# A two-block transformer kernel on one core: the gated linear recurrence's states chunk by chunk, its gates' silu apart from the copies out of PSUM, and half GEMMs written between the parts of a pair

## The chip, the core and the metric

The kernel runs on one core of a Trainium2 chip. The core has five engines that run side by side: TensorE (PE for matmuls, PEld for its weight loads), VectorE (DVE), ScalarE (ACT), GpSimd (POOL) and SyncE (SP, which only issues DMAs here). Each engine takes its own instructions strictly in order and waits on semaphores for the others. Matmul results land in PSUM, everything else is in SBUF. The metric is the device time of one execution in microseconds (us), as the median over runs.

## The reference, cut to what matters

The whole computation is two transformer blocks in float32. The first has two layers over 512 latent and 256 context positions of width 1024; the second has one layer. The change lies in one branch of the first block, which runs once in each of its two layers: a gated linear recurrence with four heads of 64 keys and 64 values, run forward and backward over the positions.

```
a     = cumsum(log f) inside a chunk
S_new = exp(a_last) * S + sum_s (k * exp(a_last - a))^T v      # one state per chunk, 64 x 64 per head
out   = (q * exp(a)) S  +  (scores inside the chunk) v
y     = rms_norm(out_forward + out_backward) * silu(gate)
```

The kernel uses chunks of 32 positions, so there are 24 chunks per direction (8 of the context, then 16 of the latent positions). The layer's other branches (attention, Fourier, convolution) have gates of their own: each is a GEMM of the normalised input with 256 columns of `w_in`, passed through silu. Layer 0 needs both streams (768 positions); layer 1 needs the branch outputs of the 512 latent positions alone.

## The kernel before, in words

Every float32 GEMM is done as three matmuls of a high and a low part (`mm3`, L187 to L191; the parts are made by `split`, L193 to L195, on ACT and DVE). Weights come as units of 256 columns: a DMA brings 1 MB, ACT writes the high parts (`wh`), DVE the low parts (`wl`). `Ahead.more` prepares the next unit while the current one is in use; there is room for about one unit of `wh` and `wl` at a time. `cp_gemm` (L457) computes one half of a unit, 128 columns, for all positions: 24 matmuls 512 wide (`gl`) and, in layer 0, 24 matmuls 256 wide (`gc`). A half is what this text calls a half GEMM.

`hgrn` (from L737) does the recurrence for two pairs of heads, j = 0 and j = 1. For each it computes the forget gates (`kk`, `lf`), and for j = 0 also the queries `q` and the values `ivt`. Then `hgrn_pair` (L807) handles the pair in four parts: two directions, each with a context part of 2 tiles (256 positions) and a latent part of 4 tiles (512 positions). A part (`hgrn_part`, L834) has two steps:

- Step one, on DVE and ACT alone: a running sum over each chunk (L843, L845), then exponentials and products that give `kt`, `F`, `Qd`, `Kd` (L853 to L889).
- Step two, with PE: `kt` is transposed (L894) and copied out (`KT`, L896); matmuls give each chunk's own update of the state (L906), three ACT instructions copy the updates into the state tile `S` (L912, L914); matmuls give the scores inside the chunks (L923), which DVE masks and adds up into `sc` (L931 to L939). Two of the four update results lie in PSUM tiles of the tag `sm`, of which there are two, and the scores need the same two.

After the two parts of a direction `hgrn_scan` (L941) turns the updates into states. Before the change the state tile is laid out as [128, 64 values, 24 chunks], with the chunks side by side; the decays are spread to 1536 columns by one copy (L946), and one scan instruction over 1536 columns (L948) runs the recurrence, with a zero decay at each row's first chunk. `hgrn_out` (L950) then multiplies `sc` with the values and the decayed queries with the states of the chunk before (both L976), squares and normalises the result (L983 to L986), and transposes bring it back (L830) to be multiplied into `y` (L832).

The gates are written around the pair. For j = 0 these are `y[4:6]` ahead of the pair, `y[2:4]` after its four parts and scans, `y[6:8]` after `hgrn_out`. For j = 1 these are `y[0:2]` after the parts, and one more unit after `hgrn_out` whose GEMM result DVE multiplies into `y[0:2]` (L803). `gate` (L993) runs two half GEMMs and lets ACT apply silu on the way out of PSUM (L998). `fill` runs one step of an independent filler, matmuls over `w_mod` (L398).

The order of instructions on each engine is not the order of the source. The framework that builds the program keeps, on every engine, a list of instructions whose inputs will be ready by its own estimate, and takes the one written first among those; so the place in the source is a rank. `ACT_TABLE_LOAD` instructions, which exchange ACT's function table between silu, sigmoid, exp and ln, are not in the source; the compiler adds them.

Of the kernel before, what the change touches and what calls it, by code (L numbers as in the profile page):

```python
# [147 lines left out]
class K:  # L148
# [588 lines left out]
    def hgrn(self, l, w_in, need, hp):  # L737
        nc = self.nc
        segs = ((0, 512), (512, 256))
        nt = 6 if need else 4  # L740
        self.hgmask = hp.tile([128, 192], I32, tag="hgmask", name="hgmask", bufs=1)
        nc.scalar.dma_start(self.hgmask, self.I["c_hgmask"])
        self.scanmask = hp.tile([128, 512], F32, tag="scanmask", name="scanmask", bufs=1)
        nc.scalar.dma_start(self.scanmask, self.I["c_scanmask"])
        ivt = hp.tile([128, 6, 256], F32, tag="ivt", name="ivt", bufs=1)
        qs = [None, None]
        for j in range(2):
            u = self.first if l == j == 0 else self.units.take()
            kk = [hp.tile([128, T], F32, tag="kk", name="kk") for _ in range(2)]
            lf = [hp.tile([128, T], F32, tag="lf", name="lf") for _ in range(2)]  # L750

            def evac(d, p, c0, n):
                nc.scalar.activation(kk[d][:, c0:c0 + n], p, AF.Sigmoid, scale=-1.0)
                nc.scalar.activation(lf[d][:, c0:c0 + n], p, AF.Sigmoid)

            for d in range(2):
                evac(d, self.cp_gemm(u[d], need_lat=False, tag=("mm" if j else "sm"))[1], 512, 256)
            if j == 0:
                ps = self.lat_gemm(u, ("mm", "mm"))
                self.units.more()  # L760
                for d, p in enumerate(ps):
                    evac(d, p, 0, 512)
            else:
                for d in range(2):
                    evac(d, self.cp_gemm(u[d], need_ctx=False, more=d == 1)[0], 0, 512)
            self.fill()
            if j == 0:
                u = self.units.take()
                for jj in range(2):
                    pl, pc = self.cp_gemm(u[jj], need_ctx=need, more=jj == 1)  # L770
                    q = hp.tile([128, T], F32, tag="q", name="q")
                    nc.scalar.activation(q[:, 0:512], pl, AF.Silu)
                    if need:
                        nc.scalar.activation(q[:, 512:768], pc, AF.Silu)
                    qs[jj] = q
                self.fill()
                for i, ps in self.tp_panel():
                    nc.scalar.activation(ivt[:, i, :], ps, AF.Copy)
                    if i in (1, 4):
                        self.fill()  # L780
            for d in range(2):
                sc_, bi = self.lscale[:, l, d, j:j + 1], self.lbias[:, l, d, j:j + 1]
                nc.scalar.activation(lf[d], lf[d], AF.Ln, scale=sc_, bias=bi)
                if l:
                    nc.vector.tensor_scalar(kk[d], kk[d], sc_, None, ALU.mult)
            self.dbg(f"lf{l}{j}0", lf[0]); self.dbg(f"lf{l}{j}1", lf[1])
            if j == 0:
                self.gate(self.y[4:6], need)
            steps = self.hgrn_pair(l, j, kk, lf, qs[j], ivt, need, nt, hp)
            next(steps)  # L790
            if j == 0:
                self.gate(self.y[2:4], need)
                next(steps)
                self.gate(self.y[6:8], need)
                next(steps, None)
            else:
                self.gate(self.y[0:2], need)
                next(steps)
                u = self.units.take()
                for jj in range(2):  # L800
                    for p, (c0, n) in zip(self.cp_gemm(u[jj], need_ctx=need, more=jj == 1), self.segs(need)):
                        ys = self.y[jj][:, c0:c0 + n]
                        nc.vector.tensor_tensor(ys, ys, p, ALU.mult)  # L803
                self.fill()
                next(steps, None)

    def hgrn_pair(self, l, j, kk, lf, q, ivt, need, nt, hp):  # L807

        nc = self.nc
        sc = hp.tile([128, 6, 2, 32], F32, tag="sc", name="sc", bufs=1)  # L810
        Ss = [hp.tile([128, 64, 24], F32, tag="S", name="S") for _ in range(2)]
        decs = [hp.tile([128, 24], F32, tag="dec", name="dec") for _ in range(2)]
        parts = [self.hgrn_part(d, c0, n, kk[d], lf[d], q, ivt, need or c0 == 0, j, Ss[d], decs[d], sc, hp)
                 for d in range(2) for c0, n in ((512, 256), (0, 512))]
# [2 lines left out]
        for n in range(4):  # L817
            if n < 3:
                next(parts[n + 1])
            next(parts[n], None)  # L820
            if n % 2:
                self.hgrn_scan(Ss[n // 2], decs[n // 2], hp)
        yield
        on = self.hgrn_out(lf, Ss, sc, ivt, nt, j, hp)
        yield
        y = self.y[4 + j]
        for (i0, n) in ((0, 4), (4, 2))[:2 if need else 1]:
            tr = self.psum("tr", [128, 128 * n])
# [5 lines left out]
    def hgrn_part(self, d, c0, n, kk, lf, q, ivt, out, j, St, dec, sc, hp):  # L834
# [66 lines left out]
        for ii in range(ntile):  # L901
            i = c0 // 128 + ii
            for A in range(4):
                rs = slice(32 * A, 32 * A + 32)
                for p in range(2):
                    nc.tensor.matmul(ups[A][64 * p:64 * p + 64, ii], KT[rs, 128 * ii + 64 * p:128 * ii + 64 * p + 64],  # L906
                                     ivt[rs, i, 128 * j + 64 * p:128 * j + 64 * p + 64], start=True, stop=True)
        sv = St[:, :, o0:o0 + nch]
        if d:
            sv = sv[:, :, ::-1]  # L910
        sv = sv.rearrange("p v (i a) -> p a i v", a=4)
        nc.scalar.activation(sv[:, 0:2], u2[:, :, :64 * ntile].rearrange("p a (i v) -> p a i v", v=64), AF.Copy)  # L912
        for A in (2, 3):
            nc.scalar.activation(sv[:, A], ups[A], AF.Copy)  # L914
# [23 lines left out]
                nc.vector.tensor_reduce(s1, M.rearrange("p i (l t) -> p i t l", l=3), AX.X, ALU.add)  # L938
                nc.vector.tensor_tensor(so, so, s1, ALU.add)  # L939

    def hgrn_scan(self, St, dec, hp):  # L941

        nc = self.nc
        nc.vector.memset(dec[:, 0:1], 0.0)
        de = hp.tile([128, 64, 24], F32, tag="de", name="de", bufs=1)
        nc.vector.tensor_copy(de, dec[:, None, :].to_broadcast([128, 64, 24]))  # L946
        S2 = St.rearrange("p v c -> p (v c)")
        nc.vector.tensor_tensor_scan(S2, de.rearrange("p v c -> p (v c)"), S2, 0.0, ALU.mult, ALU.add)  # L948

    def hgrn_out(self, Qas, Ss, sc, ivt, nt, j, hp):  # L950

# [2 lines left out]
        for i in range(nt):  # L954
            todo = {}
            for A in range(4):
                qsl = slice(32 * A, 32 * A + 32)
                for p in range(2):
                    t = [(sc[qsl, i, p, :], ivt[qsl, i, 128 * j + 64 * p:128 * j + 64 * p + 64])]
                    for d in range(2):  # L960
                        if i >= 4:
                            c = 4 * (i - 4) + A
                            c = c if d == 0 else 7 - c
                        else:
                            c = 4 * i + A
                            c = 8 + (c if d == 0 else 15 - c)
                        if c == 0:
                            continue
                        x0 = 128 * i + 32 * A
                        t.append((Qas[d][64 * p:64 * p + 64, x0:x0 + 32], Ss[d][64 * p:64 * p + 64, :, c - 1]))  # L970
                    todo[A, p] = t

            for n_ in range(3):
# [16 lines left out]
    def segs(self, need):  # L990
        return ((0, 512), (512, 256)) if need else ((0, 512),)

    def gate(self, tiles, need):  # L993

        u = self.units.take()
        for j in range(2):
            for p, (c0, n) in zip(self.cp_gemm(u[j], need_ctx=need, more=j == 1), self.segs(need)):
                self.nc.scalar.activation(tiles[j][:, c0:c0 + n], p, AF.Silu)  # L998
        self.fill()

    def attention(self, l, w_in, need, ap):
        nc = self.nc
# [1086 lines left out]
```

## Time and profile before

| what | value |
|---|---|
| median of 3 runs | 1754.92 us (1752.55 to 1758.75) |
| the profiled execution's own time | 1756.17 us |
| its span, first to last instruction | 1754.4 us |
| PE busy | 1630.6 us (93%) |
| DVE busy | 1017.9 us (58%) |
| ACT busy | 872.1 us (50%) |
| mean granted TensorE clock | 0.965 |

PE is busy for most of the span; the rest, some 124 us, is time in which PE had nothing it could start. [...] An engine's idle time is listed with the instruction that ended it, so that a row "A <- B" reads: A waited, and B let it go.

### The profile page before, as it was taken

To read this page: it belongs to the slowest core of one execution; us is meant where nothing else is said; L and a number is where in the kernel's file an instruction comes from. 1 tells how busy PE (TensorE), PEld (TensorE's weight loads), DVE (VectorE), ACT (ScalarE), POOL (GpSimd) and SP (SyncE) were. 2 spreads that over 40 slices of the span, in tenths; PEclk is the share of its full clock that TensorE was granted. 3 is DMA by queue.
4 is the path that set the end of the run, shared out by engine and by line. 5 is a ranking of instruction groups with operands and counts; after the bars stand their busy time and mean duration, and the time that the engine had idled before them with its cause. 6 is when DMAs were issued, how large, how long until landed. Compare 5 with 4: busy or idle time off the path is not lost. (4 is left out here: it accounts for less than half of the span.)

```text
span 1754.4 us, 31468 instructions
## 1 busy us (share of the span) xinstructions
PE 1630.6 (93%) x12731; PEld 1334.6 (76%) x12731; DVE 1017.9 (58%) x2133; ACT 872.1 (50%) x1754; POOL 220.4 (13%) x226
## 2 busy tenths in 40 slices
PE   5998979999999887999999889999999999999998
PEld 3876758877778675879787668777788888888886
DVE  4635473676565546586777896778766633333223
ACT  4844662553467474455556732666555533333222
POOL 2100001101230000110213443002100011111000
PEclk8998989999999898999999997999999999999999
DMA  9231203202454111213764234102724533332431
GB/s 361 104 122 51 96 27 130 98 1 67 166 161 168 51 49 56 96 49 96 265 208 135 73 90 97 37 25 70 230 85 168 181 88 99 99 99 85 156 109 72
DMA packets 162574, 193.86 MB, mean 111 GB/s; under 512 B 15054, under 2 KB 124910, under 8 KB 160252
## 3 DMA queue, kind: packets, MB, share of 16 engines
q1 hardware_dynamic: 156604, 183.37, 32.2%
q10 hardware_dynamic: 5824, 8.47, 1.7%
q8 instruction: 100, 1.64, 0.4%
q14 instruction: 46, 0.38, 0.1%
HBM read 175.28 MB, written 13.66 MB: 108 GB/s over the span
## 5 line engine op out<-in xcount | busy, mean ns | idle before, releaser
L194 ACT ACTIVATE wh<-raw 128x512 fp32r<-128x512 f32 (+1 forms) x458 | 282.3, 628 | 435.6 <-PE mm L190 161.2
L195 DVE TENSOR_TENSOR wl<-raw,wh 128x512 fp32r<-128x512 f32 x416 | 285.1, 699 | 357.7 <-ACT wh L194 344.7
L189 PE MATMUL mm<-xh,wh 128*128 128x512 f32 x520 | 208.4, 401 | 1.4 <-ACT acc L1627 1.0
L191 PE MATMUL mm<-xh,wl 128*128 128x512 f32 x520 | 208.1, 401 | 0.0
L190 PE MATMUL mm<-xl,wh 128*128 128x512 f32 x520 | 207.8, 400 | 0.0
L191 PE MATMUL gl<-xh,wl 128*128 128x512 f32 (+1 forms) x480 | 182.4, 381 | 6.0 <-DVE wl L195 3.9
L189 PE MATMUL gl<-xh,wh 128*128 128x512 f32 (+1 forms) x480 | 181.7, 379 | 3.5 <-ACT y L998 2.5
L190 PE MATMUL gl<-xl,wh 128*128 128x512 f32 (+1 forms) x480 | 180.6, 377 | 0.1
L189 PEld LDWEIGHTS mm<-xh,wh 128*128 128x128 f32 x520 | 100.6, 193 | 23.0 <-ACT acc L1627 1.9
L191 PEld LDWEIGHTS mm<-xh,wl 128*128 128x128 f32 x520 | 100.4, 193 | 20.5
L190 PEld LDWEIGHTS mm<-xl,wh 128*128 128x128 f32 x520 | 100.3, 193 | 20.5
L189 PEld LDWEIGHTS gl<-xh,wh 128*128 128x128 f32 x480 | 93.4, 195 | 22.8 <-issue 3.4
L191 PEld LDWEIGHTS gl<-xh,wl 128*128 128x128 f32 x480 | 93.9, 196 | 19.6 <-DVE wl L195 5.2
L190 PEld LDWEIGHTS gl<-xl,wh 128*128 128x128 f32 x480 | 93.5, 195 | 14.3 <-issue 1.1
L195 POOL TENSOR_TENSOR wl<-raw,wh 128x512 fp32r<-128x512 f32 x42 | 58.1, 1388 | 110.8 <-ACT wh L194 74.4
L189 PE MATMUL gc<-ch,wh 128*128 128x256 f32 x224 | 66.6, 299 | 2.6 <-ACT ch L194 2.6
L190 PE MATMUL gc<-cl,wh 128*128 128x256 f32 x224 | 66.5, 297 | 1.8 <-DVE cl L195 1.8
L190 PE MATMUL wo<-wl,yh 128*128 128x512 f32 x160 | 65.0, 407 | 3.1 <-DVE wl L195 2.9
L191 PE MATMUL gc<-ch,wl 128*128 128x256 f32 x224 | 65.8, 294 | 0.0
L191 PE MATMUL wo<-wh,yl 128*128 128x512 f32 x160 | 63.5, 399 | 0.0
L189 PE MATMUL wo<-wh,yh 128*128 128x512 f32 x160 | 63.3, 401 | 0.0
L2005 POOL TENSOR_TENSOR al<-t,ah 128x512 fp32r<-128x512 f32 x22 | 28.3, 1287 | 212.6 <-ACT ah L2004 212.6
(599 smaller groups left out, 3833.4 us busy)
## 6 DMA issues: line engine op xcount, KB each, us to landing
raw<-in_w_in SPq DMA_DIRECT2D x32, 1024.0 KB, 4.9
raw<-in_w_gate_up SPq DMA_DIRECT2D x44, 512.0 KB, 4.8
raw<-in_w_mod SPq DMA_DIRECT2D x16, 1024.0 KB, 6.5
raw<-in_w_out SPq DMA_DIRECT2D x12, 1024.0 KB, 5.4
raw<-in_w_down SPq DMA_DIRECT2D x10, 1024.0 KB, 4.9
mraw<-in_w_mod SPq DMA_DIRECT2D x8, 1024.0 KB, 12.0
raw<-in_w_out SPq DMA_DIRECT2D x16, 512.0 KB, 6.6
raw<-in_w_ckv SPq DMA_DIRECT2D x8, 1024.0 KB, 5.1
```

What stands on the lines that cost most here:

```text
L189: mm(out, ah, bh, start=start, stop=False)
L190: mm(out, ah, bl, start=False, stop=False)
L191: mm(out, al, bh, start=False, stop=stop)
L194: self.nc.scalar.activation(hi, src, AF.Copy)
L195: (eng or self.nc.vector).tensor_tensor(lo, src, hi.bitcast(F32), ALU.subtract)
L2005: nc.gpsimd.tensor_tensor(al[j], t, ah[j].bitcast(F32), ALU.subtract)
```

## The change

Five things change, all in the first block's recurrence:

- The state tile becomes [128, 24 chunks, 64 values]: a chunk's 64 values lie side by side. The three ACT copies of each part and the reads of `hgrn_out` follow that layout.
- `hgrn_scan` becomes 23 `scalar_tensor_tensor` instructions on DVE, one per chunk, each state computed from the one before. The copy of the decays and the zeroing go.
- The gates `y[0:2]`, `y[2:4]`, `y[6:8]` are copied out of PSUM without silu. Silu is written once for all six tiles, in place in SBUF, in front of the last unit of j = 1 (`conv_halves`). `y[4:6]` keep silu on the way out of PSUM.
- The two units that were written after the parts and after `hgrn_out` are cut in four half GEMMs. The first is written between the first step of the second part and the second step of the first part, the second likewise one part later, the third between the last scan and `hgrn_out`, the fourth after `hgrn_out`.
- The scratch tile that held the spread decays remains, for `hgrn_out` alone.

```diff
@@ -786,29 +786,33 @@
             self.dbg(f"lf{l}{j}0", lf[0]); self.dbg(f"lf{l}{j}1", lf[1])
             if j == 0:
                 self.gate(self.y[4:6], need)
-            steps = self.hgrn_pair(l, j, kk, lf, qs[j], ivt, need, nt, hp)
-            next(steps)
             if j == 0:
-                self.gate(self.y[2:4], need)
-                next(steps)
-                self.gate(self.y[6:8], need)
-                next(steps, None)
+
+                work = chain(self.gate_halves(self.y[2:4], need, AF.Copy), self.gate_halves(self.y[6:8], need, AF.Copy))
             else:
-                self.gate(self.y[0:2], need)
-                next(steps)
-                u = self.units.take()
-                for jj in range(2):
-                    for p, (c0, n) in zip(self.cp_gemm(u[jj], need_ctx=need, more=jj == 1), self.segs(need)):
-                        ys = self.y[jj][:, c0:c0 + n]
-                        nc.vector.tensor_tensor(ys, ys, p, ALU.mult)
+                work = chain(self.gate_halves(self.y[0:2], need, AF.Copy), self.conv_halves(need))
+            self.hgrn_pair(l, j, kk, lf, qs[j], ivt, need, nt, hp, work)
+
+    def conv_halves(self, need):
+
+        nc = self.nc
+        u = self.units.take()
+        for j, t in enumerate(self.y[0:2] + self.y[2:4] + self.y[6:8]):
+            t = t[:, :T if need else S]
+            nc.scalar.activation(t, t, AF.Silu)
+        for jj in range(2):
+            for p, (c0, n) in zip(self.cp_gemm(u[jj], need_ctx=need, more=jj == 1), self.segs(need)):
+                ys = self.y[jj][:, c0:c0 + n]
+                nc.vector.tensor_tensor(ys, ys, p, ALU.mult)
+            if jj:
                 self.fill()
-                next(steps, None)
-
-    def hgrn_pair(self, l, j, kk, lf, q, ivt, need, nt, hp):
+            yield
+
+    def hgrn_pair(self, l, j, kk, lf, q, ivt, need, nt, hp, work):

         nc = self.nc
         sc = hp.tile([128, 6, 2, 32], F32, tag="sc", name="sc", bufs=1)
-        Ss = [hp.tile([128, 64, 24], F32, tag="S", name="S") for _ in range(2)]
+        Ss = [hp.tile([128, 24, 64], F32, tag="S", name="S") for _ in range(2)]
         decs = [hp.tile([128, 24], F32, tag="dec", name="dec") for _ in range(2)]
         parts = [self.hgrn_part(d, c0, n, kk[d], lf[d], q, ivt, need or c0 == 0, j, Ss[d], decs[d], sc, hp)
                  for d in range(2) for c0, n in ((512, 256), (0, 512))]
@@ -817,12 +821,15 @@
         for n in range(4):
             if n < 3:
                 next(parts[n + 1])
+            if n < 2:
+                next(work)
             next(parts[n], None)
             if n % 2:
-                self.hgrn_scan(Ss[n // 2], decs[n // 2], hp)
-        yield
+                self.hgrn_scan(Ss[n // 2], decs[n // 2])
+        next(work)
         on = self.hgrn_out(lf, Ss, sc, ivt, nt, j, hp)
-        yield
+        for _ in work:
+            pass
         y = self.y[4 + j]
         for (i0, n) in ((0, 4), (4, 2))[:2 if need else 1]:
             tr = self.psum("tr", [128, 128 * n])
@@ -905,10 +912,10 @@
                 for p in range(2):
                     nc.tensor.matmul(ups[A][64 * p:64 * p + 64, ii], KT[rs, 128 * ii + 64 * p:128 * ii + 64 * p + 64],
                                      ivt[rs, i, 128 * j + 64 * p:128 * j + 64 * p + 64], start=True, stop=True)
-        sv = St[:, :, o0:o0 + nch]
+        sv = St[:, o0:o0 + nch]
         if d:
-            sv = sv[:, :, ::-1]
-        sv = sv.rearrange("p v (i a) -> p a i v", a=4)
+            sv = sv[:, ::-1]
+        sv = sv.rearrange("p (i a) v -> p a i v", a=4)
         nc.scalar.activation(sv[:, 0:2], u2[:, :, :64 * ntile].rearrange("p a (i v) -> p a i v", v=64), AF.Copy)
         for A in (2, 3):
             nc.scalar.activation(sv[:, A], ups[A], AF.Copy)
@@ -938,14 +945,11 @@
                 nc.vector.tensor_reduce(s1, M.rearrange("p i (l t) -> p i t l", l=3), AX.X, ALU.add)
                 nc.vector.tensor_tensor(so, so, s1, ALU.add)

-    def hgrn_scan(self, St, dec, hp):
-
-        nc = self.nc
-        nc.vector.memset(dec[:, 0:1], 0.0)
-        de = hp.tile([128, 64, 24], F32, tag="de", name="de", bufs=1)
-        nc.vector.tensor_copy(de, dec[:, None, :].to_broadcast([128, 64, 24]))
-        S2 = St.rearrange("p v c -> p (v c)")
-        nc.vector.tensor_tensor_scan(S2, de.rearrange("p v c -> p (v c)"), S2, 0.0, ALU.mult, ALU.add)
+    def hgrn_scan(self, St, dec):
+
+        nc = self.nc
+        for c in range(1, 24):
+            nc.vector.scalar_tensor_tensor(St[:, c], St[:, c - 1], dec[:, c:c + 1], St[:, c], ALU.mult, ALU.add)

     def hgrn_out(self, Qas, Ss, sc, ivt, nt, j, hp):

@@ -967,7 +971,7 @@
                         if c == 0:
                             continue
                         x0 = 128 * i + 32 * A
-                        t.append((Qas[d][64 * p:64 * p + 64, x0:x0 + 32], Ss[d][64 * p:64 * p + 64, :, c - 1]))
+                        t.append((Qas[d][64 * p:64 * p + 64, x0:x0 + 32], Ss[d][64 * p:64 * p + 64, c - 1]))
                     todo[A, p] = t

             for n_ in range(3):
@@ -990,13 +994,19 @@
     def segs(self, need):
         return ((0, 512), (512, 256)) if need else ((0, 512),)

-    def gate(self, tiles, need):
+    def gate_halves(self, tiles, need, f=AF.Silu):

         u = self.units.take()
         for j in range(2):
             for p, (c0, n) in zip(self.cp_gemm(u[j], need_ctx=need, more=j == 1), self.segs(need)):
-                self.nc.scalar.activation(tiles[j][:, c0:c0 + n], p, AF.Silu)
-        self.fill()
+                self.nc.scalar.activation(tiles[j][:, c0:c0 + n], p, f)
+            if j:
+                self.fill()
+            yield
+
+    def gate(self, tiles, need):
+        for _ in self.gate_halves(tiles, need):
+            pass

     def attention(self, l, w_in, need, ap):
         nc = self.nc
```

## Rows read from the trace of the kernel before

**Rows 1.** The page, busy time of each engine and the granted clock in 40 slices.

```profile
PE 1630.6 (93%) x12731; PEld 1334.6 (76%) x12731; DVE 1017.9 (58%) x2133; ACT 872.1 (50%) x1754; POOL 220.4 (13%) x226
PEclk8998989999999898999999997999999999999999
```

**Rows 2.** Busy time by stretch: the four pairs; last, one half GEMM of layer 0.

```profile
core 0: us, PE busy (x) PEld busy (x) DVE busy (x) ACT busy (x) POOL busy (x), PEclk, DMA share, GB/s
117.00:189.00 72.00, 63.17 (x1285) 48.41 (x1284) 36.22 (x67) 34.13 (x59) 2.66 (x2) 0.88 0.18 61
206.00:283.00 77.00, 63.93 (x1287) 48.69 (x1287) 51.76 (x104) 46.84 (x83) 3.12 (x4) 0.89 0.17 57
572.00:621.00 49.00, 41.26 (x886) 31.04 (x885) 27.82 (x43) 23.97 (x44) 2.03 (x2) 0.90 0.15 45
637.00:699.00 62.00, 45.81 (x906) 34.21 (x904) 39.91 (x68) 38.86 (x64) 2.49 (x4) 0.86 0.12 40
179.06:187.40 8.34, 8.34 (x50) 7.33 (x48) 2.41 (x4) 2.13 (x4) 0.71 (x1) 1.00 0.01 2
```

**Rows 3.** What PE waited for, 117 to 290 us: total us, times, longest.

```profile
PE sm L923 <- ACT S L914: 8.8, 10, 2.8
PE tr L894 <- DVE kt L857: 3.8, 2, 3.2
```

**Rows 4.** The same, 565 to 705 us.

```profile
PE tr L894 <- DVE kt L857: 6.9, 5, 2.8
PE sm L923 <- ACT S L914: 5.7, 8, 1.6
```

**Rows 5.** ACT in order of time, inside the first pair: start, us, instruction.

```profile
130.35 1.55 ACT L914 ACTIVATE S<-sm 128x256 f32<-128x256 f32 x2
131.92 1.28 ACT L998 ACT_TABLE_LOAD   x1
133.22 0.60 ACT L998 ACTIVATE y<-gl 128x512 f32<-128x512 f32 x1
133.83 1.28 ACT L869 ACT_TABLE_LOAD   x1
```

**Rows 6.** Line 254, in the second block's set-up: when it ran.

```profile
L254 DVE CAST identb<-early x1: 228/228/228, 4.9 to 4.9; 128x128 bf16<-128x128 f32 x1
```

**Rows 7.** ACT's copies out of PSUM by shape: xcount | busy, mean ns | idle before.

```profile
L912 ACT ACTIVATE S<-sc 128x512 f32<-128x512 f32 x8 | 11.4, 1428 | 5.1 <-PE sm L906 5.1
L914 ACT ACTIVATE S<-sm 128x256 f32<-128x256 f32 x16 | 12.4, 921 | 0.0
L896 ACT ACTIVATE KT<-tr 128x512 f32<-128x512 f32 x8 | 5.1, 638 | 2.7 <-DVE s L938 1.4 <-DVE sc L935 1.3
L896 ACT ACTIVATE KT<-tr 128x256 f32<-128x256 f32 x8 | 3.0, 373 | 2.4 <-DVE sc L935 1.7 <-PE tr L894 0.6
```

**Rows 8.** PE in order of time: one tile of hgrn_out, and L906's first passes.

```profile
167.06 0.84 PE L976 MATMUL sc<-S,lf 64*32 64x64 f32 x32
167.83 0.45 PE L976 MATMUL sc<-ivt,sc 32*32 32x64 f32 x16
168.21 0.84 PE L976 MATMUL sc<-S,lf 64*32 64x64 f32 x32
...
229.79 0.28 PE L906 MATMUL sc<-ivt,KT 32*64 32x64 f32 x4
...
230.08 0.36 PE L906 MATMUL sc<-ivt,KT 32*64 32x64 f32 x5
```

**Rows 9.** DVE's scan and its decays' copy, and the nearest rows of the new instruction.

```profile
L948 DVE TENSOR_TENSOR_SCAN S<-de,S 128x1536 f32<-128x1536 f32 x8 | 26.9, 3358 | 22.8 <-ACT S L914 22.8
L946 DVE COPY de<-dec 128x1536 f32<-128x1536 f32 x8 | 7.6, 951 | 2.3 <-ACT dec L853 2.2
L1202 DVE SCALAR_TENSOR_TENSOR cacc<-cu,col,cacc 128x770 f32<-128x770 f32 x4 | 4.1, 1014 | 0.0
L1202 DVE SCALAR_TENSOR_TENSOR cacc<-cu,col,cacc 128x512 f32<-128x512 f32 x4 | 3.0, 745 | 0.0
```

**Rows 10.** DVE in order of time: an instruction that needs the one before.

```profile
148.61 0.37 DVE L938 TENSOR_REDUCE s<-M 128x64 f32<-128x192 f32 x1
149.02 0.22 DVE L939 TENSOR_TENSOR sc<-sc,s 128x64 f32<-128x64 f32 x1
```

**Rows 11.** ACT by shape: the table loads at the gates, and a pass over one y.

```profile
L998 ACT ACT_TABLE_LOAD x12 | 15.4, 1283 | 0.2
L194 ACT ACTIVATE yh<-y 128x768 fp32r<-128x768 f32 x8 | 6.4, 835 | 2.7 <-DVE y L832 1.7 <-PE tr L1109 1.0
L194 ACT ACTIVATE yh<-y 128x512 fp32r<-128x512 f32 x8 | 4.6, 622 | 1.2 <-POOL y L1174 1.2
```

## The prediction

> **What bounds the kernel now.** I read the page first: PE is busy for 1630.6 of 1754.4 us, no other engine for more than 58% [rows 1]. [...] Next the busy time by stretch around the four pairs of the recurrence, which the change rewrites. They take 72 + 77 + 49 + 62 = 260 us, in which PE is busy for 63.2 + 63.9 + 41.3 + 45.8 = 214.2 us [rows 2]. Thus 45.8 us of the 124 lie here, and the clock is 0.86 to 0.90 against 1.00 in the half GEMM listed beside them. Nothing else binds: in the second pair, the tightest, DVE is busy for 51.8 of 77 us and ACT for 46.8, while PE has 63.9.
>
> Third, PE's waits in the pairs. The largest is the scores' matmuls behind ACT's copies of the states, 8.8 + 5.7 = 14.5 us, because both use the two `sm` tiles; the second is the transposes behind DVE's `kt`, 3.8 + 6.9 = 10.7 us [rows 3, 4]. So the delays that PE sees come from ACT and DVE being late inside the parts, not from a lack of GEMM work: the gates fill the holes already. That shows in ACT's order of time: the silu of `y[2:4]`, written behind all four parts, runs at 133.2 us between a copy of the states and the exponentials of a later part, with a table load of 1.28 us on both sides [rows 5]. The place in the source is a rank only, and it reaches far: a cast written in the second block's set-up (line 254) ran at 4.9 us [rows 6].
>
> **The state copies (ACT).** A latent part issues one copy of 512 and two of 256 columns, at 1.43 + 2 x 0.92 us; plain copies out of PSUM of these widths take 0.64 and 0.37 us [rows 7]. With contiguous values I take the latter: 3.27 falls to 1.38 us, 1.9 us less for each of 8 latent parts; the 8 context parts gain about half as much, together some 23 us of ACT. On PE's path lie only the 14.5 us of waits. A wait of one to two microseconds that loses up to 1.9 us mostly goes; I take **-9 us**, ends -14.5 and 0. Late next are the masks of DVE, one in front of each reuse of `sm`.
>
> **The state reads (PE).** In `hgrn_out` 32 passes over `S`, strided by 24 words, start within 0.77 us, and 16 over contiguous `ivt` within 0.38: 24 ns a pass for both, which says no gain. But the `ivt` passes crowd four small corners of the array, and L906, spread over eight places as the `S` passes are, starts 32 contiguous ones in 0.29 us [rows 8]. So a group of 32 falls from 0.77 us to between 0.29 and 0.77. There are 6 + 6 + 4 + 4 = 20 groups, on PE itself, with PE work queued behind: ends -9.6 and 0. I take **-6 us**, nearer to L906, whose shape of use is the nearer.
>
> **The scan (DVE).** Removed are a scan of 3.36 us and a copy of 0.95, the latter ahead of time. The new instruction is seen at 770 and 512 columns: 1014 and 745 ns, so 1.04 ns a column, and 745 - 448 x 1.04 = 278 ns at 64 [rows 9]. Each needs the one before: 148.61 + 0.37 to 149.02 shows about 35 ns between such a pair [rows 10]. 23 x 0.278 = 6.4 us of busy time, 7.2 us as a chain, in place of 4.3 busy and 3.4 in the chain. Eight scans cost DVE 17 to 23 us more. On the path lies the second scan of a pair, ahead of `hgrn_out`: 3.8 us later, four times. In front of it PE now has the third half GEMM, 8.3 us in layer 0 [rows 2], which covers it; in layer 1 the halves have no context part, and the next stage's GEMM must help. I take **+4 us**, ends 0 (all covered) and +23 (all on the path). A gain is excluded: the first tile of `hgrn_out` needs the backward direction's chunk 22, the last state but one.
>
> [...]
>
> **The later silu (ACT).** The copies out of PSUM cost as before and need no table. Silu over six tiles adds 6 x 0.835 us in layer 0 and 6 x 0.622 in layer 1, 8.7 us in all, by the row of a like pass [rows 11]. The 12 loads at the gates, 15.4 us [rows 11], would mostly go if these passes ran together at the end. I do not expect it: they carry a late rank, but each is ready when its tile is copied, and ACT, busy for 34 of 72 us in the first pair [rows 2], has holes. So they will be pulled forward singly, each with a load and one back, as in [rows 5]. Twelve passes then load about as often as now. What is gained is that PSUM is freed without a load. I take **+2 us**, ends -20 (16 loads and returns gone, all on the path) and +14 (silu and two more loads with returns, all on the path). Behind such a pass on ACT stand exponentials, `KT` and state copies, for which PE waits.
>
> **The halves (PE's order).** The GEMM work and its DMAs are the same; SP's loads keep their order, and what follows each half (the split of the next unit, on ACT and DVE, and `fill`) moves with it. The first half now outranks the first part's transposes. That covers up to 8.3 us in which `kt` is late, and takes as much fill from the rear of the pair. The 10.7 us of waits for `kt` bound it on both sides: -10.7 if all go, +10.7 if as much appears behind `hgrn_out`, where DVE and ACT normalise before the last transposes. Since the next pair's context GEMMs can also fill there, I take **-4 us**.
>
> **The clock.** It fell where PE was being kept waiting; shorter waits may spare a piece. I take **-1 us**, ends 0 and -8.
>
> **Sum.** -9 - 6 + 4 + 2 - 4 - 1 = -14 us against the profiled execution's own 1756.17 us (span 1754.4 and 1.8 around it): **1742 us**. The median shown is 1.25 us lower than that execution, within the spread of the runs, so I leave it. Of this kernel 0.3%, 5.3 us, is about what a measurement can tell from no change.
>
> **Rivals.** *The pair goes at DVE's pace (slower).* In the second pair DVE has 51.8 of 77 us; two scans bring it to some 57, while PE's own work falls. If DVE's chain, not GEMM work, ends the pairs, then the 17 to 23 us come through whole, the state copies help little since DVE is late anyway, and only the 6 us of reads and some 2 of waits come off: 1756 + 20 - 8 = 1768 us. It decides once the halves are used up before `hgrn_out` starts. For it: the waits for `kt`. Against: in three pairs DVE is busy for 50 to 65% only.
>
> *The waits move (no change).* Order is not what the source says, so the halves and the late silu do nothing, and the slower scan eats what the copies give: 1756 - 6 + 2 = 1752 us. This is the case in which the change doesn't do what it says. For it: [rows 5, 6].
>
> *Silu stays together (faster).* Then ACT is relieved by 20 us of loads and 23 of copies, and two thirds of the 25 us of the two waits go, plus the reads: 1756 - 17 - 6 - 8 (`KT`, clock) + 4 = 1729 us. [...]
>
> **How the numbers follow.** Forecast 0.40, waits move 0.22, silu together 0.20, DVE's pace 0.18. Range 1724 to 1764 us: it holds the forecast, the second and most of the third, and the cheap half of the slow one; outside lie the corners where several bounds meet. Faster by over 0.3%: nearly all of 0.40, 0.20, and a small share of 0.22, 0.63. Within: 0.19. Slower: 0.18.
>
> **What would show it.** Right: L912 at 512 columns near 0.64 us; waits of L923 for L914 under 6 us; a group of 32 `S` passes under 0.5 us; steps of 0.27 to 0.32 us in the scan; single silu passes between exponentials with loads on both sides; PE's loss in the pairs near 35 us. Wrong: silu passes in one run; L976 waiting for DVE's steps; DVE busier than PE inside a pair; lasting gaps behind `hgrn_out`.

## The result and the profile after

The changed kernel took 1737.92 us (median of 4 runs, 1735.12 to 1742.93) beside 1756.84 for the kernel before (4 runs, 1752.55 to 1759.89): ratio 0.9893, 95% interval 0.9874 to 0.9912, so 18.9 us less. The forecast was 1742. The profiled execution took 1742.93, with a span of 1740.8, the slowest of the four; the profiles stand 13.6 us apart where the medians stand 18.9.

From the page, busy time and granted clock, answering to [rows 1]. The granted clock is the share of full speed that PE was granted; every record of it in the two traces is 1.0 or 0.5 (23 of each before, 22 of each after), so a number between them is a mean.

```profile
PE 1621.8 (93%) x12731; PEld 1332.0 (77%) x12731; DVE 1027.1 (59%) x2293; ACT 860.3 (49%) x1764; POOL 222.4 (13%) x226
PEclk8999999999999988999999987999999999999999
```

PE is busy for 8.8 us less with the same 12731 matmuls; DVE has 160 instructions more. The four pairs, answering to [rows 2]; columns: stretch, length, then busy us (instructions) of PE, PEld, DVE, ACT, POOL, then the granted clock:

```profile
117.00:181.00 64.00, 56.85 (x1284) 44.34 (x1276) 37.95 (x107) 32.07 (x63) 2.58 (x2) 0.97 0.20 69
199.00:266.00 67.00, 56.61 (x1257) 44.18 (x1250) 49.05 (x136) 37.53 (x78) 1.32 (x1) 0.92 0.19 65
571.00:613.00 42.00, 34.48 (x835) 27.13 (x835) 27.01 (x79) 20.41 (x43) 1.02 (x1) 0.86 0.16 53
629.00:684.00 55.00, 43.87 (x911) 34.34 (x911) 40.95 (x106) 34.12 (x64) 2.49 (x4) 0.90 0.23 79
```

PE's loss in them is 7.15 + 10.39 + 7.52 + 11.13 = 36.2 us; the forecast said near 35, from 45.8. In no pair is another engine busier than PE. What PE waited for, 117 to 275 us and then 555 to 690 us (total, times, longest), answering to [rows 3, 4]:

```profile
PE sm L930 <- issue: 4.3, 2, 2.2
PE tr L901 <- DVE kt L864: 3.6, 2, 2.7
PE gl L190 <- issue: 2.8, 1, 2.8
PE tr L837 <- DVE big L990: 1.6, 2, 1.2
...
PE sm L930 <- ACT S L921: 1.2, 2, 0.9
```

```profile
PE sm L930 <- issue: 6.9, 5, 2.2
PE sc L913 <- ACT KT L903: 3.8, 2, 3.5
PE sc L980 <- issue: 3.2, 1, 3.2
PE tr L901 <- DVE kt L864: 2.6, 2, 1.4
PE tr L837 <- DVE big L990: 2.1, 1, 2.1
```

The wait for the state copies, 14.5 us before, is down to 1.2, and that for `kt` from 10.7 to 6.2. In their place stands "issue": PE had nothing to wait for that the trace shows, and still did not start. It was 8.1 us in the pairs before and is 19.4 now; so 8.1 of the 124 us in which PE stood still before were no lack of work that it could start. ACT's copies of the states by shape (count, busy, mean ns, 100 to 300 us), answering to [rows 7]; the state reads of `hgrn_out`, grouped and then in order of time, to [rows 8]; DVE's steps, with what ended its idle time ahead of them, to [rows 9]; one pass of the later silu, to [rows 5]:

```profile
L921 ACT ACTIVATE S<-sm 128x256 f32<-128x256 f32 x8 | 2.6, 383 | 0.0
L919 ACT ACTIVATE S<-sc 128x512 f32<-128x512 f32 x4 | 2.3, 585 | 0.3 <-PE sm L913 0.3
```

```profile
L980 PE MATMUL sc<-S,lf 64*32 64x64 f32 x624 | 9.7, 225 | 4.1 <-issue 4.1
```

```profile
169.72 0.45 PE L980 MATMUL sc<-S,lf 64*32 64x64 f32 x32
170.10 0.45 PE L980 MATMUL sc<-ivt,sc 32*32 32x64 f32 x16
```

```profile
L952 DVE SCALAR_TENSOR_TENSOR S<-S,dec 128x64 f32<-128x64 f32 x184 | 51.4, 281 | 9.6 <-ACT S L921 4.7 <-ACT S L919 1.0 <-DVE S L952 0.5
```

```profile
129.82 1.28 ACT L802 ACT_TABLE_LOAD   x1
131.11 0.85 ACT L802 ACTIVATE y<-y 128x768 f32<-128x768 f32 x1
131.97 1.28 ACT L876 ACT_TABLE_LOAD   x1
```

The signs the forecast named are all there: copies of 512 columns at 0.59 us (1.43 before), 32 state reads started within 0.38 us (0.77 before), steps of 281 ns (278 forecast), single passes of silu between exponentials with a load on both sides. One of its signs against shows a little: behind `hgrn_out` the last transposes wait for the normalisation (`big`) for 3.7 us, 1.2 before. The whole agrees too. The experiments show that the steps behind it do not.

### The profile page after: what moved, and what is told of

It reads as the page before. It is cut to its first block, busy times and chain, and to the rows that moved or that the text cites. A ratio compares the mean times of both kernels' runs of the same rounds, so it can differ in the third digit from the quotient of the medians.

```text
span 1740.8 us, 31627 instructions
## 1 busy us (share of the span) xinstructions
PE 1621.8 (93%) x12731; PEld 1332.0 (77%) x12731; DVE 1027.1 (59%) x2293; ACT 860.3 (49%) x1764; POOL 222.4 (13%) x226
## 4 chain that ended last, share of the span: by engine, by line
PE 67%; DVE 15%; ACT 8%; issue 5%; POOL 3%; DMA 2%; ACTq 0%; POOLq 0%; DVEq 0%; SPq 0%
PE mm L189 7%; PE mm L190 7%; PE mm L191 7%; PE gl L189 4%; PE gl L190 4%; PE gl L191 4%; DVE acc L1639 3%; DVE wl L195 2%; PE tr L1119 2%; PE gc L190 1%; PE tr L1109 1%; PE rg L190 1%; PE gc L189 1%; PE rg L191 1%; PE gc L191 1%
## 5 line engine op out<-in xcount | busy, mean ns | idle before, releaser
L952 DVE SCALAR_TENSOR_TENSOR S<-S,dec 128x64 f32<-128x64 f32 x184 | 51.4, 281 | 9.6 <-ACT S L921 4.7
```

The source lines that it names most:

```text
L952: nc.vector.scalar_tensor_tensor(St[:, c], St[:, c - 1], dec[:, c:c + 1], St[:, c], ALU.mult, ALU.add)
```

## The experiments

All times are ratios to the kernel before, run on the same chip, whose median was 1756.7, 1759.0 and 1756.8 us in the three sets; 0.001 is 1.76 us.

**First set: the three parts apart.** Three edits make the change, so some can be left out.

e1, the kernel before with the new states alone (layout, copies, reads, 23 steps):

```diff
-        Ss = [hp.tile([128, 64, 24], F32, tag="S", name="S") for _ in range(2)]
+        Ss = [hp.tile([128, 24, 64], F32, tag="S", name="S") for _ in range(2)]
...
+        for c in range(1, 24):
+            nc.vector.scalar_tensor_tensor(St[:, c], St[:, c - 1], dec[:, c:c + 1], St[:, c], ALU.mult, ALU.add)
```

> The kernel before with the states chunk by chunk alone: the new layout, its copies, its reads and the 23 steps; silu stays in the evacuation of the gates, the halves stay where they were. Theory A (the states make the gain: ACT's copies no longer hold the scores' matmuls, and PE's reads are shorter): 1744 us, 1740 to 1748, with the waits of the scores' matmuls for the state copies under 6 us in the four pairs. Theory B (the gain is the order of the halves, which covers what is late): within 4 us of the kernel before, 1752 to 1757. Theory C (the gain is PSUM freed without a table load, by the later silu): the same as B, 1750 to 1757 with the reads taken off.

e2, the changed kernel with silu back in the evacuation:

```diff
-work = chain(self.gate_halves(self.y[2:4], need, AF.Copy), self.gate_halves(self.y[6:8], need, AF.Copy))
+work = chain(self.gate_halves(self.y[2:4], need), self.gate_halves(self.y[6:8], need))
...
-            nc.scalar.activation(t, t, AF.Silu)
```

> The changed kernel with silu back in the evacuation of the gates' PSUM; states and halves as in the change. Theory A (the states make the gain; the later silu is worth about nothing, since its passes run singly with their loads all the same): within 3 us of the changed kernel, 1735 to 1741. Theory C (PSUM freed without a table load is what pays): 1744 us or more. If the later silu costs, as the +2 of the forecast says, 1736 us and below.

e3, the changed kernel with the halves back behind the parts:

```diff
-            if n < 2:
-                next(work)
...
         next(work)
+        next(work)
         on = self.hgrn_out(lf, Ss, sc, ivt, nt, j, hp)
```

> The changed kernel with the gates' halves back where they stood: the first two behind all four parts, the other two behind the output; states chunk by chunk and later silu as in the change. Theory A: 4 us slower than the changed kernel, 1742 us, 1739 to 1745. Theory B (the order of the halves carries the gain): 1748 us or more, with waits of the first transposes for kt as in the kernel before (10 us). If order in the source is a rank that changes little: 1738 us.

e4, the halves alone: e2 with the old layout and scan.

> The kernel before with the halves between the parts alone: old layout of the states, one scan, silu in the evacuation. Theory A: 1753 us, 1749 to 1757, with 10 us or more still lost by the scores' matmuls behind the state copies. Theory B: 1745 us or less. A rival in which the halves only take away what fills the rear of the pair: 1757 us or more.

| states | silu | halves | kernel | median us | ratio, 95% interval |
|---|---|---|---|---|---|
| new | early | behind | e1 | 1727.53 | 0.9831 (0.9811 to 0.9851) |
| new | late | behind | e3 | 1727.25 | 0.9835 (0.9818 to 0.9852) |
| new | late | between | the change | 1737.92 | 0.9893 (0.9874 to 0.9912) |
| new | early | between | e2 | 1744.73 | 0.9926 (0.9911 to 0.9942) |
| old | early | between | e4 | 1766.70 | 1.0053 (1.0039 to 1.0067) |

None of the theories A, B and C held throughout: e2 came out where C put it, but e1 contradicts C, and e4 lies where its rival, the halves missing in the rear, put it. The states alone give 29 us, more than twice what theory A said (13). The halves **cost**: 9 us on the old states, 17 on the new with early silu, 10 with late. The later silu does nothing by itself (e3 against e1) and about 6 us (interval some 1 to 10) where the halves stand between, since the change is better than e2 by 0.0033. So the best kernels are e1 and e3, 10 us below the change.

Where PE loses this is read from two stretches of each kernel, from the first value GEMM of a layer to the attention's (layer 0) or to the last transposes of the second pair (layer 1). Columns as above. Before, e1, e3, and the change:

```profile
80.80:282.50 201.70, 179.80 (x2921) 143.77 (x2917) 104.75 (x200) 103.76 (x182) 6.30 (x7) 0.92 0.23 80
541.90:698.50 156.60, 132.68 (x2085) 105.36 (x2081) 85.97 (x142) 87.55 (x150) 4.49 (x6) 0.91 0.21 69
```

```profile
80.60:263.90 183.30, 168.99 (x2919) 137.72 (x2916) 108.24 (x282) 94.71 (x182) 6.30 (x7) 0.96 0.26 88
525.90:668.70 142.80, 126.08 (x2065) 99.96 (x2061) 88.00 (x222) 78.92 (x151) 4.51 (x6) 0.94 0.24 79
```

```profile
82.90:268.40 185.50, 168.12 (x2920) 136.33 (x2917) 107.63 (x280) 92.25 (x183) 6.30 (x7) 0.96 0.25 87
529.30:672.40 143.10, 126.73 (x2094) 102.68 (x2090) 88.07 (x223) 80.62 (x156) 4.79 (x6) 0.95 0.25 82
```

```profile
80.20:269.50 189.30, 170.32 (x2921) 137.80 (x2917) 107.36 (x280) 95.09 (x185) 6.69 (x7) 0.96 0.24 85
532.00:683.50 151.50, 132.85 (x2100) 108.42 (x2096) 90.28 (x223) 84.72 (x160) 4.51 (x6) 0.92 0.25 85
```

Length less PE's busy time is what PE stood still; (1 - granted clock) x length is at most what it lost by the lower clock (to some 2 us, as the clock has two digits). In the same stretches, PE's waits by what ended them:

| us | before | e1 | e3 | the change |
|---|---|---|---|---|
| PE without work | 45.8 | 31.0 | 33.8 | 37.6 |
| lower clock, at most | 30.2 | 15.9 | 14.6 | 19.7 |
| waits for state copies | 14.5 | 2.3 | 5.4 | 1.2 |
| waits for `kt` | 10.7 | 10.3 | 11.2 | 6.2 |
| "issue" | 8.1 | 9.7 | 11.5 | 19.4 |

e1 against before: 14.8 us of standing still and up to 14.3 of clock. The waits for `kt`, which the halves were to cover, hardly moved. The change against e3: the halves did cover `kt` (5.0 us less) and the copies (4.2 less), but "issue" grew by 7.9 and the clock's share by 5.1: 3.8 + 5.1 = 8.9 us lost, against 10 measured. The "issue" of e3, all of it in these stretches:

```profile
PE sm L929 <- issue: 7.5, 4, 2.4
PE sc L979 <- issue: 2.0, 2, 1.0
PE gl L189 <- issue: 2.0, 1, 2.0
```

For e4 the same stretches give 45.1 and 27.8 us, no more than before. But its waits moved: those for `kt` (5.1 us) and for the copies (11.8) are shorter, and others grew, in part behind these stretches. In layer 1 of e4 (548 to 710.3 us), and of the kernel before (541.9 to 698.6 us):

```profile
PE sc L910 <- ACT KT L900: 8.4, 5, 4.3
PE tr L834 <- DVE big L990: 2.7, 1, 2.7
```

```profile
PE tr L830 <- DVE big L986: 1.2, 1, 1.2
```

Over the whole program PE waits for ACT's `KT` for 8.6 us in e4 (4.6 before), and the last transposes wait for the normalisation for 7.3 us (1.2 before; 7.3 in e2, 1.0 in e1). PE is also busy for 6.2 us more (1636.8 against 1630.6); why is left open.

**Second set: copies, reads, steps and loads.** Three kernels on e1, and one on the change. e5 and e6 give the steps a second tile, so that the copies alone (e5) or the reads alone (e6) go back to the old layout; e7 issues each step twice:

```diff
 e5, e6:
-            nc.vector.scalar_tensor_tensor(St[:, c], St[:, c - 1], dec[:, c:c + 1], St[:, c], ALU.mult, ALU.add)
+            nc.vector.scalar_tensor_tensor(St[:, c], St[:, c - 1], dec[:, c:c + 1], Ut[:, :, c], ALU.mult, ALU.add)
...
+            nc.vector.scalar_tensor_tensor(St[:, :, c], St[:, :, c - 1], dec[:, c:c + 1], Ut[:, c], ALU.mult, ALU.add)
 e7:
+            nc.vector.scalar_tensor_tensor(twin, St[:, c - 1], dec[:, c:c + 1], St[:, c], ALU.mult, ALU.add)
             nc.vector.scalar_tensor_tensor(St[:, c], St[:, c - 1], dec[:, c:c + 1], St[:, c], ALU.mult, ALU.add)
 e8:
-            nc.scalar.activation(t, t, AF.Silu)
+            nc.scalar.activation(t, t, AF.Silu, bias=self.zero1)
...
+                nc.vector.tensor_scalar(self.zero1, qd[:, 0:1], 0.0, None, ALU.mult)
```

> The states-alone kernel (1727.5 us) with ACT's copies put back to the old, strided layout in a tile of their own; DVE's 23 steps read it there and write the contiguous states that PE reads (one more copy of 64 columns per scan). So copies as before, reads and steps as in the change. Theory A (ACT's copies made the waits of the scores' matmuls, and each such stop of PE brought a piece at the lower clock behind it: 15 us of waits and 13 us of clock): 1743 to 1750 us, and 10 us or more of those waits again. Rival (the reads and the shorter chain make the gain, the copies' 21 us of ACT are off the path): under 1735 us.

> The states-alone kernel (1727.5 us) with the copies contiguous, while DVE's steps write states in the old layout, which PE reads strided as before (one more copy of 64 columns per scan). Theory A (the reads are PE's own time, 342 against 225 ns a group, 7 us in all): 1732 to 1738 us. Rival (the time saved there comes back as a stop of PE's instruction supply right behind): 1727 to 1730 us.

> The states-alone kernel (1727.5 us) with each of the 184 steps issued twice, the first time into a scratch tile: 51 us more of DVE, twice what the change adds. Theory A (the steps lie beside PE's work): within 4 us, 1727 to 1732, so that the change's own 17 us cost 1 us or less. Forecast's term (+4 us for 17): about 1737 to 1740. Rival of the pair at DVE's pace: 1750 us or more.

> The changed kernel (1737.9 us) with the six passes of the later silu tied behind the last exponentials of the last part (a bias of zeros worked out from them), so that they run together with one load and one back in each layer. Rival of the forecast (silu together, loads and returns off the path): 1724 to 1730 us. Theory A (the loads stand beside PE's work for the most part, some of PE's kt waits go): 1733 to 1738 us. If the run of silu holds the copies of the last part's states and the normalisation instead: 1738 us or more.

e5 gave 0.9969 (0.9955 to 0.9984), e6 0.9950 (0.9930 to 0.9970), e7 0.9992 (0.9977 to 1.0008): 24, 21 and 28 us above e1. All three give back most of the gain, and the first two are not clean, because the steps became slower. In e5, PE's waits for the copies over the whole program, and DVE's steps with their least, median and largest ns:

```profile
PE sm L924 <- ACT U L915: 15.1, 18, 2.2
L947 DVE SCALAR_TENSOR_TENSOR S<-S,dec,U x184: 344/372/380, 122.2 to 685.3; 128x64 f32<-128x64 f32 x184
```

The waits for the copies are back (15.1 us; 14.5 before, 2.3 in e1), as theory A said of e5; e6 has 2.9 us of them and lies well above both of its theories. The steps take 372 ns in place of 279 in e1, 17 us more of DVE. e7 says what that can cost: its 52 us of second steps (48 by DVE's busy time on the page, since other instructions of DVE overlap the ends of steps, in the change by 78 to 93 ns) are paid with 28, and the state reads wait for the steps, which they did not do in e1 (who waited for the second of the twin steps, us and times):

```profile
  PEld sc L975: 8.0, 5
  PE sc L975: 6.5, 3
```

So theory A's "beside PE's work" fell for e7, which came out where the rival of DVE's pace put it. e5 and e6 carry the same slow steps (medians of 372 and 374 ns), so their difference, 3 us (uncertain by some 4), is what the copies cost beyond the reads, if the prices add up; how much each costs the third set takes up.

e8 gave 0.9890 (0.9872 to 0.9908), the change's time. ACT in order of time in its first layer: one load, then six passes (four shown), with copies but no exponentials between:

```profile
244.29 1.28 ACT L802 ACT_TABLE_LOAD   x1
245.58 0.94 ACT L802 ACTIVATE y<-y,zero 128x768 f32<-128x768 f32 x1
246.48 0.60 ACT L906 ACTIVATE KT<-tr 128x512 f32<-128x512 f32 x1
246.97 2.58 ACT L802 ACTIVATE y<-y,zero 128x768 f32<-128x768 f32 x3
```

The whole program has 56 table loads in place of 68, 12 x 1.283 = 15.4 us of ACT saved, and no time is won. The six silu passes of each layer thus share one load (2 at L802, 9 in the change), and no gain shows: the loads seem to stand beside PE's work, though e8 also has 2.9 us more of "issue" than the change (22.3).

**Third set: clean doses.** On e1 again: 15 steps instead of 23 (the last eight states stay as copied); each copy of the states issued twice; reads through a strided view of the contiguous states (the values read are then not those of one chunk), which loads neither ACT nor DVE. And the change with one half less in front of the output.

```diff
 e9:
-        for c in range(1, 24):
+        for c in range(1, 16):
 e10:
+        nc.scalar.activation(tw[:, :128 * ntile].rearrange("p (a x) -> p a x", a=2), u2[:, :, :64 * ntile], AF.Copy)
...
+            nc.scalar.activation(tw[:, :64 * ntile].rearrange("p (i v) -> p i v", v=64), ups[A], AF.Copy)
 e11:
-                        t.append((Qas[d][64 * p:64 * p + 64, x0:x0 + 32], Ss[d][64 * p:64 * p + 64, c - 1]))
+                        t.append((Qas[d][64 * p:64 * p + 64, x0:x0 + 32], Ss[d].rearrange("p c v -> p (c v)")[64 * p:64 * p + 64, c - 1::24]))
 e12:
-        next(work)
         on = self.hgrn_out(lf, Ss, sc, ivt, nt, j, hp)
```

> The states-alone kernel (0.983 of the kernel before) with 15 of the 23 steps of each scan; the last 8 states are left as copied, so that part of the recurrence is left out. 15 steps of 281 ns are 4.2 us, what the old scan with its copy cost DVE, so the change's 17 to 18 us more of DVE are gone. If DVE's time has a steady price (30 us for 51 in the doubled scan): 9 to 11 us less, 0.977 to 0.978. If DVE's time is covered up to about the change's amount and only the doubled scan ran over: 0 to 3 us less, 0.981 to 0.983. Forecast's term (+4): 0.981.

> The states-alone kernel (0.983 of the kernel before) with each of ACT's copies of the states issued twice, the first time into a scratch tile, both contiguous: some 16.6 us more of ACT against the 21 us that the layout took away, and PSUM freed about as late as before; DVE and PE as in states-alone. Theory A (copies: waits of the scores, with the clock pieces behind them): 12 to 22 us slower, 0.990 to 0.996, with 8 us or more of those waits. Rival (most of ACT's time is off the path): under 5 us slower, below 0.986.

> The states-alone kernel (0.983 of the kernel before) where PE reads the contiguous states through a view of stride 24 (so the values read are not those of one chunk: the order of the states is left wrong); copies and steps as in states-alone, DVE unburdened, unlike the strided reads before. Reads as PE's own time: 7 us slower, 0.986 to 0.988. If a piece of clock or a supply stop hangs on them as well: 10 us or more, 0.989 and up. If they are hidden: within 2 us.

> The changed kernel (0.989 of the kernel before) with the third half too written behind the output: two halves between the parts, two behind the output, none right ahead of it. If the halves cost because the rear of the pair (normalisation, last transposes) has lost its fill: 5 to 8 us faster, 0.985 to 0.986. If they cost by the density of small matmuls and what the instruction supply then stops: no change or worse, 0.988 to 0.992. If the third half is needed in front of the output to cover the second scan (as the forecast said): 4 us or more slower, 0.991 and up.

| kernel | ratio, 95% interval | against its base |
|---|---|---|
| e9, 64 steps fewer (17 us of steps, 11.2 of DVE's busy time) | 0.9833 (0.9808 to 0.9858) | +0.0002, 0 us |
| e10, copies twice (18.8 us of copies, 10.1 of ACT's busy time) | 0.9875 (0.9848 to 0.9903) | +0.0044, 8 us |
| e11, strided reads | 0.9865 (0.9835 to 0.9895) | +0.0034, 6 us |
| e12, two halves in the rear | 0.9911 (0.9884 to 0.9938) | +0.0018, 3 us |

From the intervals of both, each difference is uncertain by some 6 us. e9: no gain shows, so what the change itself adds to DVE looks covered, and only more than that costs (e7). At e7's rate e9 would have given 7 to 9 us, just beyond its interval; a corner in the price of DVE's time, near which the new states sit, is thus likely, not certain, and a price of 4 us is not excluded. e10: this much of ACT's time is worth 8 us, less than theory A said, more than the rival. But the waits that theory A named hardly came back (3.5 us for the copies, 2.3 in e1), and the dose is less than what the layout took away: ACT's busy time fell by 17.1 us from the kernel before to e1 (872.1 to 855.0). e11: the reads take 6 us, the forecast's figure, but uncertain by as much; their group is the old one again (341 ns a pass on the mean, 342 in the kernel before, 225 in the change):

```profile
L973 PE MATMUL sc<-S,lf 64*32 64x64 f32 x624 | 17.6, 341 | 0.0
```

e12: not faster by 5 to 8 us as the theory of the bare rear says, and not to be told from no change. That the rear costs nothing does not follow: the last transposes still wait for the normalisation for 4.0 us (3.7 in the change), so the half that moved there did not fill it.

## Why the prediction was right, and which steps of it were not

The forecast of 1742 us lay 4 us off, on the right side and inside the range, but by errors that cancel: the states gave 29 us where the sum had 11, and the halves took 10 where it had a gain of 4. That the number came so close is luck.

- **The state reads (PE), -6.** Right: 16.8 to 9.7 us of PE in the trace, and 6 us in e11, though that run alone can hardly be told from none.
- **The state copies (ACT), -9.** Right for PE: the waits fell by 13.3 us and came back with the old copies in e5; e10 puts 8 us on 10.1 us of ACT, where the layout took away 17.1. What the step left out is the second queue that stood behind the copies. [rows 9] had it in the last column: DVE stood idle for 22.8 us in front of its 8 scans, for `S L914`. I costed the scan and the copy of its decays at their busy time, 26.9 + 7.6 us. With the idle time in front of them, 22.8 + 2.3, they took 59.6 us of DVE, and the steps in the change take 51.4 + 9.6 = 61.0. How much of the 22.8 us goes back to slow copies is not settled: e5 has the old copies, and its steps stand still for them for 9.0 us only.
- **The scan (DVE), +4.** "Eight scans cost DVE 17 to 23 us more" failed for the same reason: with the idle time counted, DVE is taken up for 1.4 us more, and by the page it is busy for 9.2 us more, as its other instructions overlap the ends of steps, by 78 to 93 ns. e9 fits with zero, and does not exclude 4. The upper end, +23, takes all eight scans, though the forecast has only four on the path, 15 us. The rival of DVE's pace is real for the doubled steps (e7); it seems to begin above the change's amount.
- **The clock, -1, ends 0 and -8.** Mis-sized. In the stretches it fell from at most 30.2 to 19.7 us in the change, and to 15.9 in e1. Where a drop is shown (last section), it lies at a stop of PE or right behind one; stops and slow time fell together in e1 and rose together with the halves on the new states, though on the old ones (e4) the clock's share did not rise.
- **The halves, -4.** Wrong in sign: +9 to +17 us. "That covers up to 8.3 us in which `kt` is late" was right (11.2 to 6.2 us). "Since the next pair's context GEMMs can also fill there" set the price in the rear below the gain: with early silu the last transposes' wait there grew by 6 us (e4 against before, e2 against e1), with late silu by 1.3 (the change against e3). The larger price in the change against e3 is in stops that I took for no resource at all, "issue", and in the clock behind them.
- **The later silu, +2.** The mechanism was right: 12 passes run singly, 68 loads against 70. Without the halves its worth is 0 (e3 against e1). With them it is some -6 us, which the profiles do not settle: PE stood still as long in e2 (20.4 + 17.4 = 37.8 us) as in the change, but e2's profiled execution is one of its fastest and the change's its slowest. The waits for `KT` and for the normalisation are 13.6 us in e2 and 7.5 in the change, and "issue" is 3.6 us longer in the change; this stays open. The rival "silu stays together" did not come about, and e8 shows that it would have given nothing, not 13 us. Of the rival "waits move" one half came: they moved, into "issue", but the time fell all the same.

The terms for reads, copies and steps, as the doses measure them, make 6 + 8 + 0 = 14 of the states' 29 us, each uncertain by some 6. The other half was not isolated. What fits is DVE's standing in front of the scan for ACT's copies (22.8 us before, 2.8 in e1, 6.1 in e10); in e1:

```profile
L945 DVE SCALAR_TENSOR_TENSOR S<-S,dec 128x64 f32<-128x64 f32 x184 | 50.5, 279 | 6.4 <-ACT S L914 2.5 <-ACT S L912 0.3
```

At the rate of e7, 28 us for 52, some 20 us of it would be worth 11. That is argued from two rates, not shown, and no run has fast copies with the single scan. The clock is a second candidate: its share in the stretches of e1 is up to 14.3 us less than before, and how much of that belongs to copies, reads or scan was not separated.

## What to carry to other kernels

Look not only at an instruction's busy time but at the idle time of its engine in front of it: in the kernel before, DVE did nothing for 22.8 us in front of its scans, nearly as long as their work (26.9). Measure the parts of a change apart even when the whole is faster: here one part of three gave 29 us, one gave 0 by itself and one took 10 back, and the kernel without it is the better one. More GEMM in a hole was not free here (9 to 17 us), where the hole lay between hundreds of tiny matmuls.

## What the runs showed of the hardware that was not expected

**PE's "issue" stops keep step with the packets of an instruction queue.** The page of the change lists the queue (packets, MB, share):

```profile
q8 instruction: 100, 1.64, 0.4%
```

12731 matmuls over 100 packets are 127 matmuls, with as many weight loads, to each 16 KB, and from matmul 7094 of the program on the packets do begin 127 matmuls apart on the mean. That they carry PE's instructions is concluded from this; the trace names no engine for them. PE's "issue" stops keep that measure. In the change, three of them (1.70 us at 586.24, 0.85 at 597.57, 3.19 at 609.32) lie 256 matmuls apart, and in e1 two (2.00 at 152.39, 0.83 at 162.42), whatever the instruction is that stands there. Counted from the program's first matmul, all eleven such stops of over 0.3 us in the change (19.1 us) keep to it: they stand before matmuls 1114, 1754, 1882, 2519, 2903 and 3159 in layer 0, and 5448, 5704, 5960, 6342 and 6726 in layer 1, within 3 of a multiple of 128 apart in each layer; and at each PE starts again 2.2 to 2.7 us after a packet of this queue began. The windows between the stops named (columns as in the stretches above; the change, then e1):

```profile
586.20:597.50 11.30, 10.48 (x256) 7.84 (x255) 7.84 (x24) 4.90 (x12) 0.00 (x0) 0.85 0.02 4
597.50:609.25 11.75, 8.55 (x256) 6.47 (x256) 5.70 (x19) 1.75 (x3) 0.00 (x0) 0.96 0.28 92
```

```profile
152.30:162.38 10.08, 9.19 (x256) 5.68 (x255) 4.78 (x15) 0.00 (x0) 0.00 (x0) 1.00 0.57 187
```

The longest of them, in order of time, and what the granted clock did during it and behind it (at six of the eleven stops the clock drops to half, between 1.0 us before the stop's end and 1.7 us after it):

```profile
609.32 0.52 PE L980 MATMUL sc<-S,lf 64*32 64x64 f32 x17 [3.19 <-issue]
```

```profile
606.10:609.30 3.20, 0.03 (x4) 0.00 (x0) 0.00 (x0) 0.00 (x0) 0.00 (x0) 0.85 0.33 114
609.30:612.00 2.70, 2.69 (x27) 2.52 (x28) 0.59 (x2) 0.38 (x1) 0.86 (x1) 0.50 0.02 6
```

PE had run the tile's reads at 12 ns a pass (32 in 0.38 us) and then stood for 3.2 us. The first 0.8 us of that were full of weight data (a load of 1 MB of `w_in`, issued at 602.86), and only then a packet of the instruction queue began; that the one held up the other is not shown (transfers by queue: packets, MB, share of 16 engines, over 100% where packets reach over the window's edge; 606.00 to 606.85 us, then 606.85 to 607.85):

```profile
q1 hardware_dynamic: 312, 0.32, 106.8%
```

```profile
q1 hardware_dynamic: 73, 0.06, 18.3%
q8 instruction: 1, 0.02, 5.5%
```

In all, 19.4 us of "issue" lie in the pairs of the change, with the clock at half (0.50 from 609.30 to 612.00 us) behind the longest stop. That the halves made them more by letting the tiny matmuls follow each other more closely is a reading of the traces; no run changed the density alone.

**The price of DVE's time may have a corner.** 17 us less of steps on DVE gave nothing that shows (e9: 0, uncertain by some 6), and 52 us more cost 28 (e7); at that rate the 17 would have given 7 to 9.
